# First product of the channel mixer by seven half products per pair of column blocks, with weight sums made partly by adding DMAs

## Chip, cores and metric

The kernel runs on one core of a Trainium2 chip. The metric is the device time of one launch in microseconds (us). The program names the engines as the profile does: PE is TensorE's matmul side, PEld its weight load, DVE is VectorE, ACT is ScalarE, POOL is GpSimd, SP is SyncE, which issues most DMAs.

## What is computed

One layer of a streaming encoder on 512 tokens with 2048 channels: an RWKV-7 token mixer, then a ConvFFN channel mixer, each between two RMS norms and modulated by the vector c. The change is in the channel mixer:

```python
def _conv_ffn(h, w_in, conv_w, conv_b, w_out):
    u = _causal_dwconv(h @ w_in, conv_w, conv_b)     # w_in: 2048 x 11008, conv of width 3
    gate, val = jnp.split(u, 2, axis=-1)             # 5504 columns each
    return (jax.nn.silu(gate) * val) @ w_out         # w_out: 5504 x 2048
...
    h = _rms(x, norm_ffn_pre[layer]) * (1 + sc_f) + sh_f
    f = _conv_ffn(h, ffn_w_in[layer], ffn_conv_w[layer], ffn_conv_b[layer], ffn_w_out[layer])
    x = x + g_f * _rms(f, norm_ffn_post[layer])
```

## The kernel before

Everything is float32 with channels on the partitions and tokens along the free dimension. A matrix product is made from 128x128 weight blocks and a 128x512 piece of the activations. Each float32 operand is split in two float32r parts, a high one (`wh`, `xh`) and the rest (`wl`, `xl`), and a block product is three matmuls: `wh`·`xh`, `wh`·`xl`, `wl`·`xh` (L246 to L248, function `mm3`). The 512 tokens are one matmul of 512 columns, or in some stages two halves of 256 (`HS`).

Weights come in 512 KB chunks of eight blocks (`w_load`, L188, issued on SP, three buffers `wr`). `w_split` makes half a chunk at a time into `wh` (a cast on ACT, L201) and `wl` (a subtraction on DVE, L203), with four buffers each, two to three halves ahead of PE.

The end of the program has these stages:

- The last six column blocks of `w_o` for half of the tokens, then for the other half (192 block products of 256 columns in all). Behind each half runs `between(h)`: norm, residual and pre-norm. Per row block it needs two DVE operations on `yo` (L1099, L1100), a square on ACT, an addition to `accx` on POOL (L1106), then a scaling on POOL (`ht`, L1116), the modulation on ACT and the split to `h2` (ACT, then DVE `xl`, L1121). At its end it stores the residual `yo` to `d_x1` by SP.
- The first three pairs of column blocks of `w_in` (a pair is block j of the gate and block j of the value) for each half of the tokens (288 matmuls of 256 columns for a half).
- Pairs 3 to 42 one after the other: 2 blocks x 16 row blocks x 3 = 96 matmuls of 512 columns a pair (`kinner`). `hidden` then makes the conv and the gating from PSUM: `conv` is one ACT and two DVE operations a block (L1157 to L1159), then silu on ACT and a DVE product into `act[j]` (L1167), which stays in SBUF. Meanwhile, from 1399 to 1525 us, `ada_jobs` multiplies the last sixth of `ada_w` by c on DVE (64 loads of 256 KB, L463).
- The product with `w_out` (`fo`): two runs of six column blocks of 512 columns, then a run of four in two halves of 256 columns, each over the 43 `act` rows, whose splits (L1246, L1247) are made four ahead. Then the last norm.

The kernel is written with a scheduling layer: the code's order is a wish, and each engine's queue is made from it ahead of time; on the chip each engine takes its queue strictly in order.

## Time and profile before

| | |
|---|---|
| median of 3 runs | 2770.28 us (2768.21 to 2771.6) |
| profiled execution (its span) | 2772.9 us |
| PE busy | 2639.9 us (95%) |
| DVE busy | 1745.4 us (63%) |
| halves of w_o, second half | 1271 to 1315 us |
| first three pairs, first and second half | 1315 to 1364 us, 1364 to 1399 us |
| pair 3 | 1399 to 1421 us |
| pairs 4 to 42 | 1421 to 2273.5 us |
| product with w_out, 512 columns | 2273.5 to 2624 us |
| product with w_out, 256 columns | 2624 to 2754 us |

The span is 2.6 us (0.1%) above the median of the timed runs, so a sum made against the span is lowered by 2.6 us to be put beside them. A row's busy time of PE counts each matmul with its latency, so the spacing of matmuls, not their mean duration, gives the rate; it is had from the number of matmuls in a stretch.

### The profile page before, as it was taken

The numbers are of one execution on the slowest core, as the hardware profiler recorded it, in microseconds if no ns is written. First come the engines' busy times: TensorE is split into PE (matmuls) and PEld (weight loads), VectorE is DVE, ScalarE is ACT, GpSimd is POOL, SyncE is SP. The second block draws the span as 40 slices with busy tenths as digits, with TensorE's granted clock in tenths as the row PEclk, the third lists the DMA queues.
The fourth block names the chain that finished last, engine by engine and source line by source line (L and its number), as shares of the span: only waits on it lengthen the run. The fifth ranks groups of instructions, "written<-read, shape, count | busy, mean of one in ns | idle before, by whom it ended". The sixth has DMA issues, their size and how long they took to land.

```text
span 2772.9 us, 40666 instructions
## 1 busy us (share of the span) xinstructions
PE 2639.9 (95%) x14946; PEld 2186.3 (79%) x14946; DVE 1745.4 (63%) x2708; ACT 1175.1 (42%) x2078; POOL 669.3 (24%) x731
## 2 busy tenths in 40 slices
PE   5899999989999999999899999999999999999997
PEld 3568787767777887788888888888888888888896
DVE  6978688888677677578877444444444454344476
ACT  4442255554444555446742333333333343343464
POOL 3543013686788464303500000000000000000000
PEclk8999999999999999999999999999999999999998
...
GB/s 303 278 200 346 252 244 204 199 199 241 185 186 204 168 183 179 120 297 192 225 220 221 99 99 95 95 99 99 95 96 99 99 90 104 99 99 93 100 207 198
DMA packets 274039, 472.28 MB, mean 170 GB/s; under 512 B 121360, under 2 KB 150416, under 8 KB 269744
## 3 DMA queue, kind: packets, MB, share of 16 engines
...
q10 hardware_dynamic: 432, 0.72, 0.1%
...
## 4 chain that ended last, share of the span: by engine, by line
PE 69%; DVE 5%; DMA 2%; issue 1%; SPq 1%; ACT 1%; POOL 0%; DVEq 0%; ACTq 0%; POOLq 0%
PE bk L246 20%; PE bk L248 20%; PE bk L247 20%; PE bk L840 2%; PE bk L871 1%; DVE wl L203 1%; PE bk L788 1%; PE bk L821 1%; PE bk L863 1%; DMA out<-x1t 1%; DMA x1t<-d_x 1%; PE bk L780 0%; PE bk L771 0%; PE bk L760 0%; PE bk L761 0%
## 5 line engine op out<-in xcount | busy, mean ns | idle before, releaser
L246 PE MATMUL bk<-xh,wh 128*128 128x512 f32 (+1 forms) x3452 | 1271.1, 372 | 7.0 <-ACT wh L201 3.3
L247 PE MATMUL bk<-xl,wh 128*128 128x512 f32 (+1 forms) x3452 | 1271.3, 370 | 0.0
L248 PE MATMUL bk<-xh,wl 128*128 128x512 f32 (+1 forms) x3452 | 1253.7, 371 | 18.4 <-DVE wl L203 18.2
L203 DVE TENSOR_TENSOR wl<-wr,wh 128x512 fp32r<-128x512 f32 x830 | 598.3, 725 | 704.9 <-ACT wh L201 681.5
L201 ACT CAST wh<-wr 128x512 fp32r<-128x512 f32 x896 | 552.2, 621 | 1087.3 <-PE bk L247 1028.0
L246 PEld LDWEIGHTS bk<-xh,wh 128*128 128x128 f32 x3452 | 655.5, 190 | 120.0 <-ACT wh L201 4.6
L248 PEld LDWEIGHTS bk<-xh,wl 128*128 128x128 f32 x3452 | 644.9, 190 | 132.8 <-DVE wl L203 23.6
L247 PEld LDWEIGHTS bk<-xl,wh 128*128 128x128 f32 x3452 | 655.3, 190 | 108.1 <-issue 3.0
L1217 POOL TENSOR_TENSOR fo<-fo,rs 128x256 f32<-128x256 f32 x4 | 3.7, 916 | 1375.2 <-ACT rs L1082 1375.2
L463 DVE SCALAR_TENSOR_TENSOR ja<-js,cs,ja 128x512 f32<-128x512 f32 x165 | 123.4, 748 | 52.9 <-DMA js<-ada 51.9
L203 POOL TENSOR_TENSOR wl<-wr,wh 128x512 fp32r<-128x512 f32 x66 | 96.5, 1464 | 96.7 <-ACT wh L201 76.4
L1247 DVE TENSOR_TENSOR xl<-act,xh 128x512 fp32r<-128x512 f32 (+1 forms) x172 | 92.1, 552 | 25.0 <-ACT xh L1246 25.0
L460 POOL TENSOR_TENSOR js<-js,cs 128x512 f32<-128x512 f32 x75 | 85.5, 1144 | 86.1 <-DMA js<-ada 67.9
L461 POOL TENSOR_TENSOR ja<-ja,js 128x512 f32<-128x512 f32 x75 | 104.6, 1395 | 2.1
L1246 ACT CAST xh<-act 128x512 fp32r<-128x512 f32 (+1 forms) x172 | 84.7, 511 | 31.9 <-PE bk L248 31.8
L712 POOL TENSOR_TENSOR ix<-ix,it 128x31 f32<-128x31 f32 (+15 forms) x124 | 90.0, 726 | 6.3
L710 POOL TENSOR_TENSOR it<-ia,ix 128x31 f32<-128x31 f32 (+15 forms) x124 | 83.3, 671 | 23.0 <-DMA ia<-d_gs 8.7
L840 PE MATMUL bk<-rh,lh 128*128 128x128 f32 x512 | 77.6, 299 | 3.5 <-DVE qz L841 2.7
L840 PEld LDWEIGHTS bk<-rh,lh 128*128 128x128 f32 x512 | 67.1, 203 | 7.8 <-DVE qz L841 3.2
L871 PE MATMUL bk<-qz,sv 128*64 128x64 f32 x512 | 63.3, 242 | 8.4 <-DVE sv L867 6.8
L396 DVE SCALAR_TENSOR_TENSOR xm<-xx,vec,h 128x512 f32<-128x512 f32 x64 | 64.0, 1058 | 9.4 <-POOL xx L382 9.4
L869 ACT ACTIVATE sv<-bk,el 64x64 f32<-64x64 f32 x128 | 39.5, 308 | 69.5 <-PE bk L863 66.3
(207 smaller groups left out, 2571.2 us busy)
## 6 DMA issues: line engine op xcount, KB each, us to landing
wr<-w SPq DMA_DIRECT2D x448, 512.0 KB
js<-ada SPq DMA_DIRECT2D x256, 256.0 KB
...
```

What stands on the lines that cost most here:

```text
L201: S.copy(hi, r)
L203: ins = on.tensor_tensor(lo, r, hi.bitcast(F32), ALU.subtract)
L246: PE.matmul(out[:, cs], wh[0:kp, 0:m], xh[0:kp, cs], start=start, stop=False)
L247: PE.matmul(out[:, cs], wh[0:kp, 0:m], xl[0:kp, cs], start=False, stop=False)
L248: PE.matmul(out[:, cs], wl[0:kp, 0:m], xh[0:kp, cs], start=False, stop=stop)
L460: G.tensor_tensor(w, w, c.to_broadcast([P, QC]), ALU.mult)
L461: G.tensor_tensor(a, a, w, ALU.add)
L463: eng.scalar_tensor_tensor(a, w, c, a, ALU.mult, ALU.add)
L712: G.tensor_tensor(X[0:BLK, j + 1:32, 0:w], X[0:BLK, j + 1:32, 0:w], tv, ALU.add)
L840: PE.matmul(qb[:, c], LH[i][:, 4 * h + c], RH[i][:, :, 4 * h + c], start=True, stop=True)
L871: PE.matmul(yp[hv, c * HD:(c + 1) * HD], sv[:, i], qz[i][:, i, q], start=True, stop=True)
L1247: V.tensor_tensor(ahl[e][1][:, cs], act[f][:, cs], ahl[e][0][:, cs].bitcast(F32), ALU.subtract)
```

## The change

Pairs 4 to 42 (`JS`, 39 of them) are computed by a Strassen scheme on a 2x2 partition: the weights of a pair are four chunks, (gate, value) x (rows 0 to 7, rows 8 to 15 of the 16 row blocks), the activations four quarters, (rows 0 to 7, rows 8 to 15) x (tokens 0 to 255, 256 to 511). Instead of eight quarter products there are seven, each of 8 row blocks x 3 matmuls of 256 columns, 168 a pair. What goes with it:

- Sums of activations (`t1`, `t2`, `t3`, `tees`), made once from `yo`, which now keeps the modulated h, and split: eight DVE operations of 1024 elements and six splits of 1024. A fourth (`tee4`) is written over the second token half of `h2[0..7]` in eight splits of 256.
- Sums of weights, for each pair: `ss[0]` and `ss[1]` by a plain load on SP (L1278) and a second DMA on POOL that adds to it (L1279, `accum_op`); `s24` by two DVE additions of 1024 elements (`f_s2`, `f_s4`). Three chunks are also loaded raw (`f_raw`). So seven 512 KB transfers a pair come in place of four, two of them adding.
- Seven weight splits of 1024 elements a pair in place of four (`f_split`); every third goes into one buffer `wx` in one piece, the others in halves as before.
- Five operations of 256 elements a pair out of PSUM on DVE and two on ACT combine the products (`u2`, `u3`, `cv`, `cg`). `hidden` reads SBUF, one product later (`late`); its last product moves to POOL, and the result is stored to DRAM (`d_act`) by POOL, except two that stay.
- The product with `w_out` starts with the two kept rows and fetches the others from `d_act` eight rows ahead. `ada_jobs` of the last sixth moves into this stage. The pool of the channel mixer is closed before it, and the new pool `outp` takes its place.
- In `between`, the residual is stored per half row block by POOL (32 stores of 128 KB) in place of 16 of 256 KB by SP, and `xt` has four buffers, not six.

```diff
@@ between(h)
             V.scalar_tensor_tensor(y, y, gm[:, kt:kt + 1], rs2[:, cs], ALU.mult, ALU.mult)
-            V.tensor_tensor(y, y, xts[kt % 6][:, cs], ALU.add)
+            V.tensor_tensor(y, y, xts[kt % NX][:, cs], ALU.add)
+            G.dma_start(d_x1[kt][:, cs], y)
...
-        if h:
-            for kt in range(KT):
-                nc.sync.dma_start(d_x1[kt], yo[kt])
-                yield
@@ hidden(j, pg, pv)
-        act[j] = ap_.tile([P, T], F32, tag=f"act{j}", name="act")
-        V.tensor_tensor(act[j], ug, uv, ALU.mult)
+        kept = {FT - 3: "xh", FT - 2: "xl"}.get(j)
+        if kept:
+            act[j] = xp.tile([P, T], F32, tag=kept, name="act", bufs=XB)
+            G.tensor_tensor(act[j], ug, uv, ALU.mult)
+        else:
+            G.tensor_tensor(ug, ug, uv, ALU.mult)
+            G.dma_start(d_act[j], ug)
@@ the sums
+    def tees():
...
+        for i in range(2):
+            while made[1] < HK + (i + 1) * n:
+                yield
+            ya, yb = big[i], big[2 + i]
+            V.tensor_tensor(ya[:, :, H0], ya[:, :, H0], ya[:, :, H1], ALU.subtract)
+            yield
+            parts_of("t1", i, ya[:, :, H0])
...
+    def f_sums(j):
+        if j in JS:
...
+            for i, (one, other) in enumerate(((2, 3), (0, 2))):
+                nc.sync.dma_start(t[:, i], chunk(j, one))
+                G.dma_start(t[:, i], chunk(j, other), accum_op=ALU.add)
+    def f_s2(j):
...
+            V.tensor_tensor(s24[0][:, 0], ss[j % 2][:, 0], l11[j], ALU.add)
+    def f_s4(j):
+        V.tensor_tensor(s24[0][:, 1], s24[0][:, 0], l12[j], ALU.add)
+    def f_split(n):
...
+        if n % 3 == 2:
...
+            hi, lo = wx[0][:, 0], wx[0][:, 1]
+            S.copy(hi, src)
+            V.tensor_tensor(lo, src, hi.bitcast(F32), ALU.subtract)
...
+    def product(n, ps, start, stop):
+        for k, (wh, wl) in enumerate(ready_w.pop(n)):
+            xh, xl = moving(n % 7, k)
+            PE.matmul(ps, wh, xh, start=start and k == 0, stop=False, skip_group_check=True)
+            PE.matmul(ps, wh, xl, start=False, stop=False, skip_group_check=True)
+            PE.matmul(ps, wl, xh, start=False, stop=k == CH - 1, skip_group_check=True)
+            tick()
@@ the pairs
-    for j in range(NF, FT):
-        pq = []
-        for q in range(2):
...
-        silu = hidden(j, *pq)
+    for m, j in enumerate(JS):
...
+        f_sums(j + 1)
+        product(n, A, True, False)
+        S.copy(p1, A)
+        f_split(n + 3)
+        if late:
+            late()
+        f_raw(l11, j + 1, 0)
+        product(n + 1, B, True, False)
+        V.tensor_tensor(u2, B, p1, ALU.subtract)
+        f_split(n + 4)
+        f_s4(j)
+        product(n + 2, C, True, False)
+        f_split(n + 5)
+        product(n + 3, B, False, False)
+        V.tensor_tensor(u3, B, p1, ALU.subtract)
+        V.tensor_tensor(cv[:, H1], u3, C, ALU.subtract)
+        f_split(n + 6)
+        f_raw(l12, j + 1, 1)
+        product(n + 4, A, False, True)
+        S.copy(cg[:, H0], A)
+        f_s2(j + 1)
+        f_split(n + 7)
+        product(n + 5, B, False, True)
+        V.tensor_tensor(cv[:, H0], B, p1, ALU.subtract)
+        f_split(n + 8)
+        f_raw(l22, j + 1, 3)
...
+        product(n + 6, C, False, True)
+        V.tensor_tensor(cg[:, H1], C, u2, ALU.subtract)
+        f_split(n + 9)
...
+    exps(late())
+    ffn.close()
+    ap_ = ctx.enter_context(tc.tile_pool(name="outp", bufs=1))
@@ the product with w_out
+    def fetch_act(i):
+        if i < FT and act[rows[i]] is None:
...
+            nc.sync.dma_start(act[f], d_act[f])
```

Three places of the engines' queues show what stands where. The names in the rows are tiles; what is in brackets is what an instruction waits for (an engine's or a DMA queue's semaphore).

DVE, in the second half of the first three pairs. Before, splits of weights (`wl`) and of `h2` (`xl`) take turns:

```order
L1121 TENSOR_TENSOR xl<-hu,xh 128x256 [waits Activation_49]
L203 TENSOR_TENSOR wl<-wr,wh 128x512 [waits DMAHW4_49,PE_49,Activation_49]
L203 TENSOR_TENSOR wl<-wr,wh 128x512 [waits DVE_49,PE_49,Activation_49]
L1121 TENSOR_TENSOR xl<-hu,xh 128x256 [waits Activation_49]
L203 TENSOR_TENSOR wl<-wr,wh 128x512 [waits DVE_49,DMAHW5_49,PE_49,Activation_49]
```

Now the sums (L1215, L1220, L1225, L1230) and their splits (L1209) stand between them:

```order
L222 TENSOR_TENSOR wl<-wr,wh 128x512 [waits DMAHW4_49,PE_49,Activation_49]
L1209 TENSOR_TENSOR t1l<-yo,t1h 128x1024 [waits Activation_49]
L1151 TENSOR_TENSOR xl<-yo,xh 128x256 [waits Activation_49]
L222 TENSOR_TENSOR wl<-wr,wh 128x512 [waits PE_49,Activation_49]
L1151 TENSOR_TENSOR xl<-yo,xh 128x256 [waits Activation_49]
L1220 TENSOR_TENSOR yo<-yo 128x4x256 [waits Activation_49]
L222 TENSOR_TENSOR wl<-wr,wh 128x512 [waits DMAHW5_49,PE_49,Activation_49]
```

Twelve of these fourteen operations of 1024 elements stand ahead of the first weight split of pair 3's own chunks, among the weight splits of this stage.

DVE, in the middle of the pairs. Before, a pair is eight weight splits and five operations of the conv:

```order
L203 TENSOR_TENSOR wl<-wr,wh 128x512 [waits DMAHW0_49,PE_49,Activation_49]
L203 TENSOR_TENSOR wl<-wr,wh 128x512 [waits PE_49,Activation_49]
L1158 SCALAR_TENSOR_TENSOR uv<-bk_16792,fvec,uv 128x511 [waits Activation_49]
L1159 SCALAR_TENSOR_TENSOR uv<-bk_16792,fvec,uv 128x510 [waits DVE_49]
L1167 TENSOR_TENSOR act<-ug,uv 128x512 [waits DVE_49]
L203 TENSOR_TENSOR wl<-wr,wh 128x512 [waits DMAHW1_49,PE_49,Activation_49]
```

Now (with the buffers' numbers), from the end of a pair's fourth product to a little behind its sixth:

```order
L1373 TENSOR_TENSOR u3_14394<-bk4_19056,p1_14392 128x256 [waits PE_49]
L1374 TENSOR_TENSOR cv_19059<-u3_14394,bk5_19057 128x256 [waits DVE_49]
L1315 TENSOR_TENSOR wl_19201<-s24_14376,wh_19200 128x512 [waits Activation_49]
L1288 TENSOR_TENSOR s24_14376<-s24_14376,wr_19204 128x1024 [waits DMAHW0_49,DVE_49]
L1305 TENSOR_TENSOR wx_14386<-wr_19108,wx_14386 128x1024 [waits PE_49,Activation_49]
L1315 TENSOR_TENSOR wl_19260<-s24_14376,wh_19259 128x512 [waits PE_49,Activation_49]
L1382 TENSOR_TENSOR cv_19059<-bk4_19056,p1_14392 128x256 [waits PE_49]
L1315 TENSOR_TENSOR wl_19264<-s24_14376,wh_19263 128x512 [waits Activation_49]
L1182 SCALAR_TENSOR_TENSOR uv_19343<-cv_19059,fvec_68,uv_19343 128x511 [waits Activation_49]
L1315 TENSOR_TENSOR wl_19295<-ss_14357,wh_19294 128x512 [waits PE_49,Activation_49]
L1285 TENSOR_TENSOR s24_14376<-ss_14397,wr_19349 128x1024 [waits DMAHW2_49,DMASW2_49,DVE_49]
```

The sums of weights have been moved far ahead: the last row (`f_s2`) is that of the pair after the next one. It stands between the ends of a pair's sixth and seventh product and waits for that later pair's adding DMA (`DMASW2_49`).

SP, in the middle of the pairs. Before, one row stands for 140 weight loads:

```order
L188 DMA wr<-w 128x1024 x140
```

Now each pair has three raw loads and the two plain loads of the sums, in this order:

```order
L1269 DMA wr<-w 128x1024 [waits DMAHW0_49,DVE_49]
L1269 DMA wr<-w 128x1024 [waits DMAHW6_49,DMAHW1_49,DVE_49]
L1269 DMA wr<-w 128x1024 [waits DMAHW7_49,DMAHW2_49,DVE_49]
L1278 DMA ss<-w 128x1024 [waits DMASW2_49,DVE_49]
L1278 DMA ss<-w 128x1024 [waits DMASW4_49,DVE_49]
```

The third of them takes the buffer that a weight split of the running pair gives free, and the loads of the sums for the pair after the next one stand behind it. At the start of the product with `w_out` SP has:

```order
L207 DMA wr<-w 128x1024 [waits DMAHW4_49,DVE_49]
L1453 DMA act<-d_act_11476 128x512 [waits DMASW3_49,DMASW4_49,DMASW2_49,DMASW5_49,DMASW1_49,DMASW6_49,DMASW0_49,DMASW7_49,PE_49,Pool_49]
L1453 DMA act<-d_act_11477 128x512
L1453 DMA act<-d_act_11478 128x512
```

The first fetch of a row waits for PE, POOL and all eight queues of POOL's DMAs, which free the closed pool's memory.

## Rows read from the trace of the kernel before

**Rows 1.** Page: busy time by engine; and the chain that ended last.
```profile
PE 2639.9 (95%) x14946; PEld 2186.3 (79%) x14946; DVE 1745.4 (63%) x2708; ACT 1175.1 (42%) x2078; POOL 669.3 (24%) x731
...
PE 69%; DVE 5%; DMA 2%; issue 1%; SPq 1%; ACT 1%; POOL 0%; DVEq 0%; ACTq 0%; POOLq 0%
```

**Rows 2.** Stretches (start:end length, busy us of each engine with instructions, clock, DMA share, GB/s).
```profile
1271.50:1315.40 43.90, 37.43 (x294) 35.70 (x293) 39.31 (x66) 28.43 (x65) 21.30 (x21) 1.00 0.54 173
1315.40:1364.50 49.10, 39.44 (x295) 37.86 (x293) 43.40 (x71) 33.14 (x76) 30.36 (x31) 0.93 0.75 241
1364.50:1399.20 34.70, 34.58 (x288) 34.58 (x289) 25.84 (x42) 26.02 (x54) 7.98 (x11) 1.00 0.62 186
1399.20:1421.00 21.80, 21.80 (x98) 18.07 (x98) 21.43 (x35) 12.89 (x20) 0.00 (x0) 1.00 0.61 190
1421.00:2273.50 852.50, 852.50 (x3777) 706.35 (x3777) 396.49 (x578) 275.23 (x442) 0.00 (x0) 1.00 0.37 113
2273.50:2624.30 350.80, 350.80 (x1549) 290.49 (x1548) 145.99 (x221) 134.76 (x229) 0.00 (x0) 1.00 0.32 98
2624.40:2686.00 61.60, 61.60 (x515) 61.60 (x514) 44.68 (x90) 41.78 (x94) 0.00 (x0) 1.00 0.61 186
```

**Rows 3.** Groups by line, 1530 to 2250 us (busy us, mean ns, idle before).
```profile
L247 PE MATMUL bk<-xl,wh 128*128 128x512 f32 x1060 | 412.4, 389 | 0.0
L203 DVE TENSOR_TENSOR wl<-wr,wh 128x512 fp32r<-128x512 f32 x265 | 183.1, 691 | 416.1 <-ACT wh L201 416.1
L1158 DVE SCALAR_TENSOR_TENSOR ug<-bk,fvec,ug 128x511 f32<-128x511 f32 x33 | 24.8, 750 | 0.0
```

**Rows 4.** The same, 1364.5 to 1399.2 us.
```profile
L246 PE MATMUL bk<-xh,wh 128*128 128x256 f32 x96 | 26.5, 284 | 1.0 <-ACT wh L201 1.0
L203 DVE TENSOR_TENSOR wl<-wr,wh 128x512 fp32r<-128x512 f32 x27 | 21.1, 795 | 8.2 <-ACT wh L201 7.2 <-PE bk L248 0.8
```

**Rows 5.** The same, whole span, shapes apart.
```profile
L1247 DVE TENSOR_TENSOR xl<-act,xh 128x512 fp32r<-128x512 f32 x86 | 57.5, 686 | 23.6 <-ACT xh L1246 23.6
L1247 DVE TENSOR_TENSOR xl<-act,xh 128x256 fp32r<-128x256 f32 x86 | 34.6, 417 | 1.4 <-ACT xh L1246 1.4
L1246 ACT CAST xh<-act 128x512 fp32r<-128x512 f32 x86 | 51.3, 620 | 28.1 <-PE bk L248 28.1
L503 POOL DMA_DIRECT2D d_xr<-xm x16 | 8.7, 541 | 15.2 <-DVE xm L502 14.6 <-issue 0.3
L661 POOL DMA_DIRECT2D d_e<-v x16 | 14.2, 887 | 42.3 <-ACT wh L201 25.9 <-ACT v L272 16.2 <-issue 0.2
```

**Rows 6.** Timeline of PE behind its longest wait (start, us, idle before).
```profile
1344.75 1.23 PE L248 MATMUL bk<-xh,wl 128*128 128x256 f32 x4 [3.53 <-DVE wl L203]
1345.77 0.41 PE L246 MATMUL bk<-xh,wh 128*128 128x256 f32 x1
1345.99 0.41 PE L247 MATMUL bk<-xl,wh 128*128 128x256 f32 x1
...
1349.70 0.28 PE L247 MATMUL bk<-xl,wh 128*128 128x256 f32 x1
```

**Rows 7.** Stretches: busiest DMA, and one 512 KB weight load from its issue.
```profile
1200.00:1225.00 25.00, 25.00 (x116) 20.81 (x115) 18.46 (x29) 7.55 (x14) 0.00 (x0) 1.00 0.95 338
1703.60:1704.60 1.00, 1.00 (x7) 0.81 (x6) 0.03 (x1) 0.00 (x0) 0.00 (x0) 1.00 0.00 0
1704.60:1706.90 2.30, 2.30 (x12) 1.91 (x11) 0.69 (x1) 0.62 (x1) 0.00 (x0) 1.00 0.69 228
```

**Rows 8.** Timeline of DVE and SP around that load.
```profile
1702.94 0.69 DVE L203 TENSOR_TENSOR wl<-wr,wh 128x512 fp32r<-128x512 f32 x1 [2.03 <-ACT wh L201]
...
1703.66 5.77 SPq L188 DMA_DIRECT2D wr<-w  x2
```

**Rows 9.** DMA issues by line (KB each, us to landing).
```profile
d_tn<-ix POOLq DMA_DIRECT2D x4, 512.0 KB, 4.6
...
d_tt<-ia POOLq DMA_DIRECT2D x4, 512.0 KB, 6.2
```

More of the change, by code (lines that the diff above doesn't have):

```diff
@@ L22 @@
 NL, NF = 6, 3
+NP = 1
 HS = (slice(0, T // 2), slice(T // 2, T))
@@ L178, in body @@
     mods = {q: cp.tile([P, KT], F32, name=f"mod{q}") for q in (2, 3, 4, 5)}
-    wst = {"load": 0, "split": 0, "use": 0, "raw": {}, "half": {}, "pool": 0}
+    wst = {"load": 0, "split": 0, "use": 0, "raw": {}, "half": {}, "pool": 0, "end": g.mid}
     def w_load():
         c = wst["load"]
-        if c >= g.nchunks:
+        if c >= wst["end"]:
             return
@@ L1179, in body, with chunk, f_raw @@
     nb = 2 * NF
-    jobs = ada_jobs(ap_, all_of(5), 7, (2,) * 6 + (1, 2), 3, last=True)
-    sides.append(jobs)
     for j in range(NF):
         hidden(j, pf[2 * j], pf[2 * j + 1])
-    for j in range(NF, FT):
+    JS = list(range(NF + NP, FT))
+    ss, s24, wx = {}, [], []
+    l11, l12, l22 = {}, {}, {}
+    def chunk(j, i):
+        return ap["w"][g.mid + 4 * (j - JS[0]) + i]
+    def f_raw(d, j, i):
+        if j in JS:
+            d[j] = wp.tile([P, CH * P], F32, tag="wr", name="wr", bufs=3)
+            nc.sync.dma_start(d[j], chunk(j, i))
@@ L1185, in body @@
+    for j in range(NF, NF + NP):
         pq = []
@@ L1236, in body @@
         b0 += n
-    steps = [(f, run[4]) for run in runs for f in range(FT)]
+    rows = out_rows(FT)
+    steps = [(f, run[4]) for run in runs for f in rows]
+    place = {f: i for i, f in enumerate(rows)}
+    def fetch_act(i):
+        if i < FT and act[rows[i]] is None:
+            f = rows[i]
+            act[f] = ap_.tile([P, T], F32, tag=f"act{f}", name="act")
+            nc.sync.dma_start(act[f], d_act[f])
+    for i in range(8):
+        fetch_act(i)
     ahl = {}
@@ L1249, in body @@
     nb = 0
-    for r, (b0, n, h, end, cs) in enumerate(runs):
+    for r, (b0, n, h, end, cols) in enumerate(runs):
         pf = [bank((nb + i) % 8) for i in range(n)]
```

200 lines of the change are left out of this document (159 added, 41 removed).

## The prediction

> **What bounds the kernel now.** I read the page first: PE is busy 95% of the span and 69% of the chain that ended last lies on it; DVE, the next engine, has 63% [rows 1]. An average hides stages, so I then cut the end of the program into stretches [rows 2]. In the 852.5 us of pairs 4 to 42 PE never pauses, the clock is granted in full, DVE works 396 us and ACT 275 us, and DMA is at 0.37. PE alone sets the time there. The halves before it are different: between 1271 and 1364 us PE idles 6.5 and 9.7 us while DVE is at about 90%.
>
> The rate of PE has to be read from spacing. At 512 columns three lines of 1060 matmuls share 720 us [rows 3], 226.4 ns each, and 1548 in 350.8 us give 226.6 [rows 2]. So 96 matmuls of a pair take **21.75 us**. (The stretch of the pairs holds 3744 of these and some 33 tiny ones of `ada_jobs`, which make up the rest of it and move with `ada_jobs` at the same price.) At 256 columns, 514 matmuls take 61.6 us and 288 take 34.6 us [rows 2]: 120 ns, not half of 226.5. PEld is busy for all of these stretches, but for only 83% of the 512-column ones: with short matmuls the weight load is what PE waits on.
>
> **The pairs, on PE.** 168 matmuls at 120 ns are **20.16 us**, a gain of 1.59 us a pair (7%, where the operation count falls by 12.5%), 39 x 1.59 = **62 us**. By the Trainium skill (TensorE: Matmul & The Clock Gate, Back-to-back issue gap) matmuls of 256 and 512 columns stand 262 and 518 cycles apart, about 109 and 216 ns; as an estimate from that page the pair would fall from 20.7 to 18.3 us and the gain would be 94 us. The trace disagrees at both widths, and the measurement decides.
>
> **The pairs, on the other engines.** *DVE:* a split of 512 costs 0.69 us [rows 3]; 256 elements take 0.42 and 512 take 0.69 [rows 5], so 1024 about 1.22. Seven splits, on average 4.67 in halves and 2.33 whole: 6.4 + 2.8. Two additions for `s24`: 2.4. Five operations of 256: 2.1. Four of the conv at 0.75 [rows 3]: 3.0. Together 16.8 us in 20.16, 83%, where it was 46%. It stays hidden only if the queue's waits don't add up. In the queue DVE must wait for PE at `u2`, `u3`, `cv` and for `wx`, whose one buffer comes free with a product; laid out against products of 2.88 us each, the order has about 2 us of slack a pair, and splits are done two products before use. I take nothing. *ACT:* seven splits at most 1.24 us each (two of 0.62, [rows 5]) and some 2.5 us else: 11 of 20 us. *POOL:* one product and three DMA issues of 0.54 to 0.89 us [rows 5]: idle otherwise. *DMA:* 3.9 MB in 20 us are 195 GB/s; 338 were reached [rows 7].
>
> **The adding DMA** is what the trace of before does not show, and it lies in a loop. `f_s2` for the pair after next waits for it in DVE's strict order. Behind `f_s2` DVE needs 9.0 to 10.3 us (12 or 13 operations, by the prices above) to come to the split that frees the buffer of the last raw chunk; only then SP issues that chunk and behind it the plain load of `ss`; the add follows that load; `f_s2` follows the add. From SP's issue (1703.66, at the end of the DVE split) to the first byte 1.0 us [rows 7, 8]. Two loads of 512 KB one behind the other: 4.6 us at the pace of the lone one (2.3 us), 3.1 us at 338 GB/s [rows 7]. The add from issue to landing: plain POOL transfers of this size took 4.6 and 6.2 us [rows 9], and if its data take twice the 2.3 us, up to 8.5. The loop is 9.0 + 1.0 + 3.1 + 4.6 = 17.7 us at the least and 10.3 + 1.0 + 4.6 + 8.5 = 24.4 at the most. I take 9.4 + 1.0 + 3.9 + 5.5 = 19.8, just under PE's 20.16, since the rows that price the add come from stretches with other traffic. So the pair stays at 20.16, but with hardly any room.
>
> **The entries and exits**, all costs. (a) 32 stores of `d_x1` on POOL, 0.54 to 0.89 us each [rows 5], stand between its additions to `accx`; POOL is 21.3 of 43.9 and 30.4 of 49.1 us busy [rows 2], and each half's norm waits for the last addition. 16 stores delay it by 9 to 14 us, of which PE has cover for most of the wait: 4 us, between 0 and 14. Storing `d_x1` by SP goes; it was hidden. (b) In 1364 to 1399 us DVE has 25.8 us of work [rows 2]; twelve operations of 1.22 us raise it to 40.5 against 34.7: **+6**, between 0 and 10. (c) From the first weight split of pair 3 to the one that the second product needs stand 38 DVE operations (12 splits, 14 of the conv, 8 of `tee4`, 4 of 1024): 8.3 + 10.5 + 3.4 + 4.9 = 27.1 us, against 21.75 + 2.9 on PE: +2.5, between 0 and 8. `ada_jobs` on DVE, which filled this stretch (21.4 of 21.8 us, [rows 2]), leaves it; that is the room it uses. (d) The first fetched `act` row waits until the closed pool is free: the last pair's conv and silu (about 4.5 us), the POOL product and its store's landing (some 6), then its own load (2 to 3.3) and split (1.3), about 14 us. The two kept rows cover 36 matmuls, 8.2 us. +6, and 2 more because PE ran at half pace for about 4 us after a wait of 3.5 us (210 ns a matmul instead of 120, from 1345.77 until 1349.6, [rows 6]): **+8**, between 0 and 12. (e) `ada_jobs` in the `w_out` stage adds 48 us of DVE work beside 146 in 351 us, and its loads and the fetched rows 27 MB beside 98 GB/s [rows 2]: nothing; without that cover the pace of DVE would show, some 10 us.
>
> **Sum.** Against the profiled span: 2772.9 - 62 + 4 + 6 + 2.5 + 8 = 2731.4. The timed runs lie 2.6 us lower: **2728 us**, 1.5% faster.
>
> **Rivals.** *1, slower: the adding loop sets the pair.* If the data of an add take twice as long, 9.4 + 1.0 + 4.6 + 7 = 22 us a pair, 0.25 more than before: 2772.9 + 10 + 20.5 - 2.6 = **2801 us**. From 20.16 us on the loop eats the gain, and from 21.2 (the gain per pair equals the 20.5 us of entries over 39) the kernel is slower than before. For it: the loop's upper half lies there. Against it: a store from POOL moved the same bytes in 4.6 us in busier stretches. The Trainium skill (Collectives: The Full Stack, The bandwidth ceiling) puts a reducing DMA at half the rate of a copy, since it reads two sources; no row of before shows an add, and this rival is what that rule would do here. *2, DVE sets the pair.* Where POOL works beside it, a split took 0.795 us, not 0.691 [rows 4]; with 15% on all its work DVE needs 19.3 us, and with 1.5 us of waits for PE 20.8: 2772.9 - 37 + 20.5 - 2.6 = **2754 us**. For it: 83% in a strict queue. Against it: POOL works little in the pairs. *3, the entries hide.* PE idles in the halves already, and the scheduler has room before pair 3; with 5 us in all **2713 us**.
>
> **Chances.** Forecast 0.48, rival 1 0.25, rival 2 0.20, rival 3 0.07. About 0.2%, 5.5 us, is what a measurement can tell from no change. The forecast, rival 3 and nearly all of rival 2 are faster than that, some of rival 1 (loops of 20.8 to 21.3 us) falls within it: faster 0.72, same 0.06, slower 0.22. The range reaches from 2708 (most entries hidden) to 2787 (a loop of 21.6 us), and leaves out 0.07 below and some 0.13 above.
>
> **What would show it.** Right: in the pairs matmuls 120 ns apart, a pair in 20.2 us, PE without pauses, `f_s2` not waiting for POOL's DMA; DVE 80 to 85% there; pauses of PE near 1315 to 1365 us, at the second product of pair 4, and 8 us into the `w_out` stage. Wrong: PE pauses in every pair, released by a split behind `f_s2` (rival 1, with DVE idle before L1285) or by a split with DVE busy throughout (rival 2); or a matmul spacing other than 120 ns.

## The result

The changed kernel took **2797.94 us** (median of 4 runs, 2791.99 to 2807.16) where the kernel before took 2769.24 on the same chip (4 runs, 2764.53 to 2771.6): ratio 1.0103, 95% interval 1.0078 to 1.0129. It is 1.0% slower; forecast were 2728 us and 1.5% faster, range 2708 to 2787. The number is that of rival 1 (2801 us). Its mechanism was only half right, as the runs below show. Once the wait is taken away by one more buffer, the same scheme takes 0.9906 of the time before (0.9887 to 0.9926).

The page of the kernel after, busy time by engine and the chain that ended last, by engine and by line [rows 1]:

```profile
PE 2602.2 (93%) x17754; PEld 2283.0 (82%) x17754; DVE 2057.6 (74%) x3103; ACT 1323.3 (47%) x2313; POOL 840.9 (30%) x925
...
PE 32%; DMA 13%; DVE 9%; issue 5%; ACT 2%; POOL 0%; DVEq 0%; SPq 0%; ACTq 0%; POOLq 0%
DMA wr<-w 10%; PE bk L267 7%; PE bk L265 7%; PE bk L266 7%; PE bk L1330 4%; PE bk L1328 4%; PE bk L1329 4%; DVE wx L1305 2%; DMA js<-ada 2%; DVE wl L1315 1%; DVE wl L222 1%; DVE ja L482 1%; DVE uv L1183 1%; DVE yo L1128 0%; DVE ug L1182 0%
```

PE had 69% of the chain and has 32%. First by line is a transfer, `wr<-w`: the load of a raw weight chunk. All DMA together had 2% before. In stretches of the program (length, busy us of PE, PEld, DVE, ACT, POOL with instructions, clock, DMA share, GB/s), cut at the same matmuls in each kernel: up to the last `w_o` blocks; from there to the first product of pair 4, which is the entry; the 39 pairs; the rest. After:

```profile
0.00:1221.87 1221.87, 1131.35 (x7323) 896.50 (x7324) 933.96 (x1420) 563.22 (x974) 607.29 (x661) 0.98 0.69 221
1221.87:1428.60 206.73, 177.13 (x1266) 167.01 (x1265) 174.54 (x266) 123.88 (x257) 82.18 (x103) 0.92 0.67 215
1428.60:2284.70 856.10, 808.75 (x6554) 798.78 (x6554) 646.53 (x889) 409.93 (x654) 142.91 (x152) 0.99 0.64 176
2284.70:2796.00 511.30, 484.96 (x2618) 420.73 (x2616) 302.57 (x530) 226.30 (x429) 8.54 (x10) 0.98 0.53 178
```

The pairs, where 62 us were to be gained, take 856.1 us against 852.5 before [rows 2]: 21.95 us a pair, not 20.16. 39 x 20.16 = 786.2 us, so 69.9 us are lost there. 47.4 us of them are time without a matmul (856.10 less 808.75). Of the other 22.5 us, some 8 are still the pauses (busy time counts each matmul with its latency, 0.28 us at a spacing of 0.12, so the starts before and behind a pause lie 0.16 us further apart than its idle time says). About 9 us are matmuls at half pace: behind six of the pauses some 100 matmuls in all stand 0.21 us apart. The rest is many short gaps. The entry is taken up behind the run of the kernel before that shows its own stretches. What PE and DVE waited for in the pairs (us, times, longest):

```profile
DVE s L1285 <- DMA wr<-w: 82.8, 37, 4.4
DVE s L1288 <- DMA wr<-w: 70.8, 28, 4.4
...
PE bk L1330 <- DVE wx L1305: 28.0, 14, 3.6
PE bk L1330 <- DVE wl L1315: 12.6, 15, 1.1
```

L1285 is `f_s2`, L1288 is `f_s4`. DVE stands still there for 153.6 us, 3.9 us a pair, and PE then waits for splits. Both are put down to a raw chunk (`l11` for `f_s2`, `l12` for `f_s4`), none to the adding DMA. One turn of the loop from one `f_s2` to the next, in order of time (start, us, engine, line, operation, idle before and its releaser):

```profile
1873.72 1.23 DVE L1285 TENSOR_TENSOR s<-ss,wr 128x1024 f32<-128x1024 f32 x1 [0.52 <-DMA wr<-w]
...
1880.55 0.85 POOL L1279 DMA_DIRECT2D ss<-w  x1 [17.87 <-DVE u L1367]
...
1881.11 0.33 SPq L1269 DMA_DIRECT2D wr<-w  x1
...
1883.60 0.90 POOL L1279 DMA_DIRECT2D ss<-w  x1
...
1886.67 0.68 DVE L1315 TENSOR_TENSOR wl<-wr,wh 128x512 fp32r<-128x512 f32 x1
...
1887.39 0.33 SPq L1269 DMA_DIRECT2D wr<-w  x1
...
1888.98 1.23 DVE L1288 TENSOR_TENSOR s<-s,wr 128x1024 f32<-128x1024 f32 x1 [1.62 <-DMA wr<-w]
...
1895.88 1.23 DVE L1285 TENSOR_TENSOR s<-ss,wr 128x1024 f32<-128x1024 f32 x1 [4.13 <-DMA wr<-w]
...
1899.27 1.22 DVE L1305 TENSOR_TENSOR wx<-ss,wx 128x1024 fp32r<-128x1024 f32 x1
...
1900.55 0.58 PE L1330 MATMUL bk<-t1h,wx 128*128 128x256 f32 x1 [2.81 <-DVE wx L1305]
```

The stretch behind that pause:

```profile
1900.55:1903.50 2.95, 2.95 (x14) 2.95 (x15) 2.95 (x6) 1.49 (x3) 0.00 (x0) 0.50 0.63 190
```

Read it as a loop. `f_s2` runs at 1873.72. DVE then works through its queue for 13.6 us until the split that ends at 1887.35 frees a raw buffer; SP loads it again at once (1887.39). Beside two adds (1880.55 and 1883.60) this load takes until 1895.9, 8.5 us, and the next `f_s2`, far ahead in DVE's queue, waits for just that chunk; by the trace, the add that it also needs had landed at 1888.7. `f_s4` at 1888.98 waited in the same way for the raw load issued at 1881.11. From one `f_s2` to the next it is 22.16 us. The split behind it comes late, PE pauses 2.81 us and runs at half pace until 1903.5, 14 matmuls in 2.95 us at a granted clock of 0.50, the lower of its two levels (1.2 GHz).

The turns are not all alike; three kinds follow one another. By the trace, 37 of the 38 turns between two `f_s2` end with the raw load; from an `f_s2` to the issue of that load it is 13.7 to 18.2 us, 15.9 in the mean (2.3 of it idle, mostly `f_s4` waiting for its own raw load), and the load takes 9.1 to 3.4 us, 5.9 in the mean. Over all raw loads of the pairs the median from issue to landing is 7.8 us. A plain load without adds beside it, some 20 us earlier, released POOL 3.9 us after its issue:

```profile
1854.90 0.33 SPq L1278 DMA_DIRECT2D ss<-w  x1
...
1858.83 0.85 POOL L1279 DMA_DIRECT2D ss<-w  x1 [17.54 <-DMA ss<-w]
```

With 3.9 us in place of 8.5 the turn shown would take 17.5 us, an estimate, under PE's 20.16.

### The profile page after: what moved, and what is told of

Read it like the earlier page. It is cut to its first block, busy times and chain, and to the rows that moved or that the text cites. A ratio compares the mean times of both kernels' runs of the same rounds, so it can differ in the third digit from the quotient of the medians.

```text
span 2796.0 us, 47774 instructions
## 1 busy us (share of the span) xinstructions
PE 2602.2 (93%) x17754; PEld 2283.0 (82%) x17754; DVE 2057.6 (74%) x3103; ACT 1323.3 (47%) x2313; POOL 840.9 (30%) x925
## 3 DMA queue, kind: packets, MB, share of 16 engines
q1 hardware_dynamic: 267776, 436.85, 49.2%
## 4 chain that ended last, share of the span: by engine, by line
PE 32%; DMA 13%; DVE 9%; issue 5%; ACT 2%; POOL 0%; DVEq 0%; SPq 0%; ACTq 0%; POOLq 0%
DMA wr<-w 10%; PE bk L267 7%; PE bk L265 7%; PE bk L266 7%; PE bk L1330 4%; PE bk L1328 4%; PE bk L1329 4%; DVE wx L1305 2%; DMA js<-ada 2%; DVE wl L1315 1%; DVE wl L222 1%; DVE ja L482 1%; DVE uv L1183 1%; DVE yo L1128 0%; DVE ug L1182 0%
## 5 line engine op out<-in xcount | busy, mean ns | idle before, releaser
L265 PE MATMUL bk<-xh,wh 128*128 128x512 f32 (+1 forms) x2204 | 782.2, 364 | 17.5 <-ACT xh L1150 5.0
L266 PE MATMUL bk<-xl,wh 128*128 128x512 f32 (+1 forms) x2204 | 786.2, 360 | 6.3 <-DVE xl L1151 6.3
L267 PE MATMUL bk<-xh,wl 128*128 128x512 f32 (+1 forms) x2204 | 768.3, 361 | 13.4 <-DVE wl L222 12.5
L220 ACT CAST wh<-wr 128x512 fp32r<-128x512 f32 x584 | 356.3, 619 | 525.4 <-PE bk L266 432.4
L222 DVE TENSOR_TENSOR wl<-wr,wh 128x512 fp32r<-128x512 f32 x518 | 386.4, 754 | 201.2 <-ACT wh L220 182.9
L1279 POOL DMA_DIRECT2D ss<-w x78 | 68.1, 873 | 689.6 <-DMA ss<-w 284.2
L1330 PE MATMUL bk<-xh,wl 128*128 128x256 f32 x832 | 237.5, 286 | 11.9 <-DVE wl L1315 11.9
L1328 PE MATMUL bk<-xh,wh 128*128 128x256 f32 x832 | 237.4, 285 | 3.8 <-DVE cv L1374 1.8
L1329 PE MATMUL bk<-xl,wh 128*128 128x256 f32 x832 | 236.4, 284 | 0.0
L1315 DVE TENSOR_TENSOR wl<-wr,wh 128x512 fp32r<-128x512 f32 x156 | 129.3, 853 | 1.3 <-ACT wh L1314 1.1
L1330 PE MATMUL bk<-xh,wx 128*128 128x256 f32 x416 | 118.6, 285 | 0.7 <-DVE wx L1305 0.5
L1328 PE MATMUL bk<-xh,wx 128*128 128x256 f32 x416 | 118.0, 284 | 0.0
L1329 PE MATMUL bk<-xl,wx 128*128 128x256 f32 x416 | 117.9, 283 | 0.0
```

The costliest lines, as they stand in the source:

```text
L220: S.copy(hi, r)
L222: ins = on.tensor_tensor(lo, r, hi.bitcast(F32), ALU.subtract)
L265: PE.matmul(out[:, cs], wh[0:kp, 0:m], xh[0:kp, cs], start=start, stop=False)
L266: PE.matmul(out[:, cs], wh[0:kp, 0:m], xl[0:kp, cs], start=False, stop=False)
L267: PE.matmul(out[:, cs], wl[0:kp, 0:m], xh[0:kp, cs], start=False, stop=stop)
L1279: G.dma_start(t[:, i], chunk(j, other), accum_op=ALU.add)
```

## Experiments on the pairs

Four explanations were open: the place of `f_s2` and `f_s4` in DVE's queue with the few raw buffers (A); the adding DMAs, as a load on the DMA engines or as a wait (B); DVE's amount (C); and, later, whether the loop goes through the raw load (R) or through the add itself (L).

**Without the adds** (`no_add`):

```diff
                 nc.sync.dma_start(t[:, i], chunk(j, one))
-                G.dma_start(t[:, i], chunk(j, other), accum_op=ALU.add)
```

> Leaves out the two adding DMAs of a pair (the sums hold their first chunk alone); the loads by SP, DVE's work and the products stay. In the changed kernel a pair takes 21.95 us where the matmuls alone are 20.16, and DVE stands idle 3.9 us a pair at f_s2 and f_s4, put down to the raw chunk's load. Theory A (place: f_s2 and f_s4 stand so far ahead in DVE's queue that the raw chunk, whose buffer comes free late, cannot have landed): the raw loads are issued as late as before, so most of the wait stays, pair 21.2 to 21.9 us, 2770 to 2795 us. Theory B (adding DMAs: beside them a raw load of 512 KB lands in 8.6 us where one alone takes 3.4): the wait is gone, pair 20.2 to 20.4, 2725 to 2735 us. Theory C (DVE has too much to do, 16.6 us a pair in a strict queue): pair 21.9, 2795 us.

Measured: 2740.17 us, the kernel before beside it 2779.74. The pairs take 786.75 us, 20.17 each. At the two sums (L1284 and L1287 in this kernel) DVE waits 6.8 us in all for raw chunks, 0.2 us a pair, and the median raw load takes 3.9 us:

```profile
1442.65:2229.40 786.75, 786.52 (x6553) 786.29 (x6552) 640.85 (x888) 416.80 (x654) 86.11 (x78) 1.00 0.43 142
```

C falls: DVE does 16.4 us a pair, nearly the 16.6 of the kernel after, and hides. B holds so far by the pairs; the time lies above its 2725 to 2735 us because the part of the program ahead of the change ended late here, at 1240.9 us.

**The same bytes by a plain transfer** (`plain_pool`):

```diff
-                G.dma_start(t[:, i], chunk(j, other), accum_op=ALU.add)
+                G.dma_start(t[:, i], chunk(j, other))
```

> The two adding DMAs of a pair become plain transfers of the same bytes by the same queue, at the same place and with the same waits (the sums then hold one chunk and are wrong). Theory B in its first form (adding is what costs): as without them, pair 20.2 to 20.5, 2725 to 2740 us, and the transfer lands in 3 to 5 us, not 9.1. Theory B in its second form (the bytes, or POOL's queue, cost): pair 21.5 to 22, 2780 to 2798 us, landing near 9 us. Theory A: 21.2 to 21.9, 2770 to 2795 us.

Measured: 2734.05 us (before 2779.74). 790.5 us for the pairs, 20.27 each. The expectation that a plain transfer lands in 3 to 5 us was wrong: it takes 7.2 us on this queue. The pair and the time are as B in its first form had them. Some of DVE's wait stays:

```profile
DVE s L1288 <- DMA wr<-w: 28.9, 22, 3.0
...
DVE s L1285 <- DMA wr<-w: 26.5, 30, 3.1
```

That is 1.4 us a pair in place of 3.9; PE waits for DVE for 2.5 us in all. The bytes alone make the raw loads late (6.45 us in the median), but not by enough.

**The two sums kept at their written place** (`pin`), with all adds:

```diff
-        V.tensor_tensor(u2, B, p1, ALU.subtract)
+        at = V.tensor_tensor(u2, B, p1, ALU.subtract)
         f_split(n + 4)
-        f_s4(j)
+        with tc.issue_after(at.ins):
+            f_s4(j)
...
-        V.tensor_tensor(cv[:, H1], u3, C, ALU.subtract)
+        at = V.tensor_tensor(cv[:, H1], u3, C, ALU.subtract)
...
-        f_s2(j + 1)
+        with tc.issue_after(at.ins):
+            f_s2(j + 1)
```

> Adding DMAs as they are; f_s4 is kept behind u2 of its own pair and f_s2 behind cv's second half, where the text has them, so that on DVE each stands 5 to 15 us later. Theory A: the raw chunk is there in time, DVE's idle time at f_s2 and f_s4 falls from 3.9 us a pair to under 0.5, pair 20.2 to 20.5, 2725 to 2740 us. Theory B (the loop over the adding DMA is itself 22 us long): the wait only moves, pair 21.5 to 22, 2780 to 2798 us. Theory C: pair 21.9, 2795 us.

Measured: 2736.34 us (before 2779.74); 788.0 us for the pairs, 20.2 each:

```profile
1438.20:2226.20 788.00, 786.52 (x6553) 786.30 (x6552) 662.80 (x891) 419.37 (x655) 143.85 (x152) 1.00 0.69 191
```

A holds as well, with the adds in full (DMA share 0.69, higher than the 0.64 of the kernel after, since the same bytes move in less time). So neither A nor B is the cause alone; the wait needs both.

**A fourth raw buffer** (`rot4`), taken in turn with the three:

```diff
+            if loads[0] % 4 == 3:
+                d[j] = ap_.tile([P, CH * P], F32, tag="wq", name="wq")
+            else:
-            d[j] = wp.tile([P, CH * P], F32, tag="wr", name="wr", bufs=3)
+                d[j] = wp.tile([P, CH * P], F32, tag="wr", name="wr", bufs=3)
+            loads[0] += 1
```

> A fourth buffer for the raw chunks, taken in turn with the three; nothing else is changed. Theory A in the form that the buffer is what comes late: raw loads are issued a third of a pair (7 us) earlier, DVE's idle time at f_s2 and f_s4 falls from 3.9 us a pair to under 1.5, pair 20.3 to 20.9, 2730 to 2755 us. Theory A in the form that the place on DVE alone matters, and theory B: SP's order puts the loads behind those of ss all the same, pair 21.5 to 22, 2780 to 2798 us.

Measured: 2734.34 us (before 2779.74); the pairs take 786.5 us, 20.17 each:

```profile
1436.00:2222.50 786.50, 786.45 (x6553) 786.24 (x6552) 646.76 (x887) 416.67 (x653) 138.36 (x152) 1.00 0.69 191
```

The buffer was the scarce thing: with the loads started earlier, `f_s2` and `f_s4` may stand where they are. DVE still waits 25.3 us at `f_s2` (0.6 a pair), which PE doesn't feel.

**The sums without their raw operand** (`no_raw`): three buffers, all loads and adds as in the kernel after, but `f_s2` and `f_s4` wait for no raw chunk.

```diff
-            V.tensor_tensor(s24[0][:, 0], ss[j % 2][:, 0], l11[j], ALU.add)
+            V.tensor_tensor(s24[0][:, 0], ss[j % 2][:, 0], ss[j % 2][:, 0], ALU.add)
...
-        V.tensor_tensor(s24[0][:, 1], s24[0][:, 0], l12[j], ALU.add)
+        V.tensor_tensor(s24[0][:, 1], s24[0][:, 0], s24[0][:, 0], ALU.add)
```

> The changed kernel with its three raw buffers, all loads and both adding DMAs of a pair; only f_s2 and f_s4 no longer read a raw chunk (each adds its first operand to itself, so the sums are wrong). Theory R (the loop that takes 21.95 us goes through the raw loads: a raw chunk is read by a split, its buffer is loaded again beside the adds in 5 to 9 us, and f_s4 or f_s2 waits for just that load): DVE's idle time at the two lines falls from 3.9 us a pair to under 1, the pair to 20.2 to 20.7 us, 2725 to 2750 us. Rival L (the loop goes through the adding DMA, issue to landing 9.1 us, and f_s2 waits for that as soon as the raw load is not later): f_s2 waits for POOL's transfer instead, pair 21.3 to 22 us, 2770 to 2798 us.

Measured: 2731.74 us (before 2769.36); 788.5 us for the pairs, 20.2 each, and the adds still land only 8.6 us after their issue:

```profile
1432.90:2221.40 788.50, 787.00 (x6553) 786.39 (x6552) 653.35 (x890) 419.32 (x654) 140.42 (x152) 1.00 0.70 191
...
ss<-w POOLq DMA_DIRECT2D x74, 512.0 KB, 8.6
```

DVE waits at neither line. R holds and L falls: the loop over the adding DMA, which the prediction had priced and rival 1 was built on, has room even with an add of 8.6 us. The loop that set the pair went through the raw load.

What an add costs the DMA engines can be read from three of these runs, from POOL's queue over the pairs (packets, MB, share of the 16 engines). Without adds, only the stores of `act` are on it:

```profile
q0 software_dynamic: 3040, 9.96, 3.4%
```

With the two transfers a pair as plain ones (`plain_pool`):

```profile
q0 software_dynamic: 13696, 48.77, 18.1%
...
ss<-w POOLq DMA_DIRECT2D x74, 512.0 KB, 7.2
```

And as adds (`pin`):

```profile
q0 software_dynamic: 13696, 48.77, 31.5%
...
ss<-w POOLq DMA_DIRECT2D x74, 512.0 KB, 7.9
```

The same packets and bytes take 31.5 - 3.4 = 28.1% as adds and 14.7% as plain transfers, 1.9 times as much engine time, while the landing grows only from 7.2 to 7.9 us (8.6 in `no_raw`, 9.2 in the kernel after). By the Trainium skill (Collectives: The Full Stack, The bandwidth ceiling) a reducing DMA runs at half the rate of a copy; the 1.9 in engine time agrees. By the Trainium skill (DMA: Bandwidth & Descriptors, Issuing engines are not separate DMA queues) transfers started by different engines run on the same 16 DMA engines and interleave; the raw load of SP that took 8.5 us beside POOL's adds agrees.

## Experiments on the entry and the end

**The kernel before once more** (`before_again`), for its stretches:

> The kernel before, once more, for its stages on this chip. In the two executions seen so far the first product's stage begins at 1421.06 us (before) and 1428.64 us (after), 7.6 us apart; but counted back by matmuls, the stretch from the last blocks of the mixer's output product to there took 184.8 us before and 206.8 after, and what lies ahead of it 1236.3 and 1221.9. If the part ahead only varies from execution to execution: it begins anywhere from 1222 to 1245 us here, the stretch takes 184 to 186 us again, and the entries of the change cost 22 us, not 7.6. If the change made the part ahead faster: it begins at 1236 to 1245 us here, where changed kernels stand at 1222 to 1241.

Measured: 2774.07 us (2771.4 beside it), and:

```profile
0.00:1235.96 1235.96, 1138.61 (x7323) 902.15 (x7324) 935.74 (x1422) 562.63 (x974) 602.63 (x661) 0.97 0.70 221
1235.96:1422.30 186.34, 172.66 (x1267) 166.57 (x1266) 158.35 (x257) 118.39 (x247) 59.58 (x62) 0.95 0.66 208
...
2275.00:2772.30 497.30, 477.56 (x2585) 415.37 (x2584) 256.32 (x453) 218.07 (x418) 6.68 (x8) 0.99 0.42 128
```

The entry takes 184.8 and 186.3 us in the two executions of before and 206.7 after: the change costs 20 to 22 us there, and not the 7.6 us that the starts of the pairs (1428.6 and 1421.06) suggest. In the six other executions here that have the same entry, with adds or plain transfers on POOL, it took 202.2 to 206.4 us, so 16 to 22 us over all. The part ahead of it, the same work in all kernels, ended at 1221.9 us in the execution of the kernel after and hid 14 us. In the other profiled executions of kernels with the change it ended between 1227 and 1241, six of the eleven by 1231, in both of before at 1236. That scatter is larger than most effects looked for here, so from here on stretches are compared, not times. Whether the change also makes that part a little faster is open.

The entry in four pieces, after (second half of the last `w_o` blocks; first three pairs, first and second token half; pair 3), for [rows 2]:

```profile
1258.69:1308.29 49.60, 38.85 (x291) 35.90 (x289) 39.75 (x66) 27.74 (x65) 24.61 (x36) 0.91 0.69 223
1308.29:1362.64 54.35, 40.35 (x289) 38.35 (x289) 46.62 (x72) 32.79 (x73) 35.45 (x46) 0.85 0.57 184
1362.64:1405.67 43.03, 38.43 (x288) 37.44 (x289) 39.06 (x50) 29.83 (x58) 15.70 (x16) 0.94 0.53 155
1405.67:1428.60 22.93, 22.93 (x97) 18.93 (x97) 19.61 (x31) 15.66 (x28) 6.41 (x7) 0.94 0.77 239
```

Before they took 43.4, 48.6 (50.1 in the second execution), 34.7 and 21.8: +6.2, +4.3 to 5.8, +8.4 and +1.1 us. In the same six other executions the third piece took 41.1 to 43.7 us and pair 3 21.6 to 22.8, so up to 3 and 1 us of these two costs are scatter.

Part of the third piece is the same effect as in the pairs. At its end PE stands for a cast that waits for a raw chunk:

```profile
1404.00 0.62 ACT L220 CAST wh<-wr 128x512 fp32r<-128x512 f32 x1 [4.87 <-DMA wr<-w]
...
1404.67 0.50 PE L265 MATMUL bk<-xh,wh 128*128 128x512 f32 x1 [2.63 <-ACT wh L220]
```

That chunk was issued at 1396.47, beside the first two adds (1395.98 and 1397.19), and took 7.5 us. In `no_add` this wait of PE isn't there, and the piece is the shortest of all kernels with the change:

```profile
1381.39:1421.11 39.72, 37.75 (x289) 36.97 (x290) 39.04 (x50) 29.43 (x58) 13.81 (x14) 0.94 0.46 150
```

**`d_x1` stored by ACT's queue** (`r4_act`, with four raw buffers):

```diff
-            G.dma_start(d_x1[kt][:, cs], y)
...
                 G.tensor_tensor(accx[:, cs], accx[:, cs], sq, ALU.add)
+            S.dma_start(d_x1[kt][:, cs], y)
```

> Four raw buffers, and the 32 stores of d_x1 issued by ACT's queue and not by POOL's. In the kernel with four raw buffers the two stretches of the halves take 50.2 and 53.8 us (43.4 and 48.6 before). Theory E1 (the stores stand between POOL's additions to accx and delay both norms): they fall to 44 to 47 and 49 to 51 us, and PE's waits for accx (6.7 us in two) fall under 3. Rival E2 (DVE's work or the two fewer x tiles set them): 49 to 51 and 53 to 55 us; or worse where ACT, busy 60% there, becomes the bound.

Measured: 2734.48 us (before 2771.4). The first three pieces (the fourth took 22.96 us):

```profile
1265.92:1309.79 43.87, 38.47 (x290) 36.74 (x289) 36.81 (x63) 26.56 (x61) 18.57 (x19) 0.96 0.73 225
1309.79:1361.82 52.03, 39.77 (x290) 38.50 (x288) 44.27 (x75) 33.83 (x77) 30.91 (x30) 0.89 0.64 206
1361.82:1411.00 49.18, 41.19 (x288) 39.16 (x288) 41.57 (x52) 31.12 (x60) 17.57 (x18) 0.90 0.60 181
```

The first piece is back at 43.9 us and PE's waits for `accx` are gone: E1 holds there. The second piece takes 52.0 us, where 53.8 were to become 49 to 51: little of it was the stores. And with four buffers alone the third piece took 43.3 us and now it takes 49.2; the sum of the four falls only from 170.0 to 168.0. So the gain is given back in the piece where DVE makes the token sums. What DVE does there is argued as the cause, not shown: it runs almost without a pause from 1361.8 to 1398, and it is slower beside POOL. While POOL works (first row) an operation of 1024 elements takes 1.75 us, with POOL idle 1.21; one of 256 takes 0.96 and 0.41. ACT also waits longer for raw chunks there, 11.5 us against 7.3 with four buffers alone.

```profile
1363.95 3.29 POOL L1146 TENSOR_TENSOR ht<-yo,rs 128x256 f32<-128x256 f32 x3 [0.17 <-ACT yo L1147]
1364.89 1.75 DVE L1215 TENSOR_TENSOR yo<-yo 128x1024 f32<-128x1024 f32 x1
...
1370.06 0.96 DVE L1151 TENSOR_TENSOR xl<-yo,xh 128x256 fp32r<-128x256 f32 x1
...
1374.11 0.41 DVE L1151 TENSOR_TENSOR xl<-yo,xh 128x256 fp32r<-128x256 f32 x1
...
1387.04 1.21 DVE L1230 TENSOR_TENSOR yo<-yo 128x1024 f32<-128x1024 f32 x1
```

**Second parts of the sums on POOL** (`r4_tp`, with four raw buffers): in `tees` alone

```diff
-            V.tensor_tensor(lo, src, hi.bitcast(F32), ALU.subtract)
+            G.tensor_tensor(lo, src, hi.bitcast(F32), ALU.subtract)
```

> Four raw buffers, and six of the fourteen large operations that make the token sums (the second parts, 1024 columns each) are done by POOL and not by DVE. The second half of the first product's first columns took 34.65 us before and 43.3 with four raw buffers, where PE waits for DVE's weight splits. Theory (DVE's amount sets it): 37 to 40 us. Rival (POOL's operations are slow and slow down DVE beside them, or delay h2): 43 us or more, and the first pair's second product may wait for the sums, 1 to 5 us more there.

Measured: 2740.12 us (before 2771.4); the third piece takes 47.8 us in place of 43.3, beyond its scatter. The rival holds: work given to POOL lengthens the piece.

**Half of the sums later, behind a second ordinary pair** (`r4_np2g`, with four raw buffers):

```diff
-NP = 1
+NP = 2
...
             while made[1] < HK + (i + 1) * n:
                 yield
+            while i and not go:
+                yield
...
     for j in range(NF, NF + NP):
+        if j == NF + NP - 1:
+            go.append(j)
```

(each step of `tees` is also kept behind the last weight split written before it.)

> Four raw buffers; two pairs in the ordinary way ahead of the seven-product ones and not one, and the second half of the token sums (seven operations of 1024 columns, 8.5 us of DVE) held back until the second of them. With four raw buffers the second half of the first columns takes 43.3 us with DVE at 90%, where PE needs 34.65, and the ordinary pair 22.8 where it needs 21.6. Theory (DVE's amount there sets the entry): the half takes 35 to 38.5 us, the two ordinary pairs 21.6 to 22.3 each; against four buffers alone the entry gains 5 to 8 us and the second ordinary pair costs 1.6, so 3 to 6 us less in all. Rival (the norm's latency and the weight splits set it, not the sums): 42 us or more, and 0 to 2 us more in all.

Measured: 2750.86 us (before 2769.36), of which 10 us is a slow first part (it ended at 1239.9). The third piece takes 40.9 us, between the 35 to 38.5 of the theory and the 42 of the rival; from the start of the entry to the end of the second ordinary pair it is 226.7 us, which is what four buffers alone need for the entry and their first seven-product pair (206.4 + 20.5). So nothing is gained in all, as the rival has it. With seven operations fewer the piece is 2.4 us shorter than with four buffers alone, hardly below its scatter (41.1 to 43.7), so DVE's amount is not what sets it.

**Both together** (`best`):

> Four raw buffers, d_x1 stored by ACT's queue, two ordinary pairs and the second half of the token sums held back. If the two cures of the entry add up (6 us in the first half by the stores, 5 to 8 in the second by the sums, less 1.6 for the second ordinary pair): 2720 to 2728 us where the kernel before takes 2770, ratio 0.982 to 0.985. If DVE's amount over the whole entry is what counts, so that a gain at one place is lost at the next: 2728 to 2735 us, ratio 0.985 to 0.987. In neither case slower than before.

Measured: 2737.72 us (median of 4, 2730.82 to 2744.98), ratio 0.9885 (0.9859 to 0.9912). The entry to the end of the second ordinary pair takes 222.0 us, 4.8 less than with four buffers alone, but the 38 pairs behind it take 3.4 us more and the rest 2.3. The cures don't add up, and the time lies above both expected ranges. What holds the third piece at 46.5 us there, with DVE busy for 34.6 of them, no run takes away. The trace has one candidate: ACT waits 11.6 us for raw chunks there, and PE's longest wait behind the start of the piece (2.80 us at 1402.95) is for a cast whose chunk took 9.1 us, while the second add was in flight (1391.90 to 1401.99).

**The last hidden unit kept in SBUF** (`r4_keep`, with four raw buffers):

```diff
-        kept = {FT - 3: "xh", FT - 2: "xl"}.get(j)
+        kept = {FT - 3: "xh", FT - 2: "xl", FT - 1: "xh"}.get(j)
```

> Four raw buffers, and the last hidden unit is kept in a slot of the first product's operand instead of going through memory. With four raw buffers alone PE stands still for 4.4 us where the first fetched act row is due; that row is asked for at 2230.95 us, 0.5 us behind the landing of the last store (2230.42, issued 2228.08), and the part from the end of the pairs to the end takes 510.0 us (499.4 before, about 4 us of it moved work). Theory X1 (the closed pool is free when that store has landed): the row is asked for 2.5 to 3 us earlier, PE's wait falls to 1 to 2 us, the part to 505 to 508. Rival X2 (another user of the pool, PE or DVE, is as late): no change within 1 us.

Measured: 2737.82 us (before 2771.4). With four raw buffers alone the first row is asked for at 2230.95, 8.4 us behind the end of the pairs (2222.5); a kept row had been split long before:

```profile
2218.30 1.29 DVE L1471 TENSOR_TENSOR xl<-act,xh 128x512 fp32r<-128x512 f32 x2
...
2228.08 0.59 POOL L1196 DMA_DIRECT2D d_act<-ug  x1 [0.30 <-POOL ug L1195]
...
2230.95 0.33 SPq L1458 DMA_DIRECT2D act<-d_act  x1
```

With the last unit kept, 5.2 us behind it (2223.6), at the end of POOL's product and not of a store:

```profile
2227.53 1.26 POOL L1193 TENSOR_TENSOR act<-ug,uv 128x512 f32<-128x512 f32 x1 [17.65 <-ACT ug L1188]
...
2228.82 0.33 SPq L1458 DMA_DIRECT2D act<-d_act  x1
2229.41 1.29 DVE L1471 TENSOR_TENSOR xl<-act,xh 128x512 fp32r<-128x512 f32 x2 [2.69 <-ACT xh L1470]
```

X1 is right on the fetch, which comes 3.2 us earlier. But the kept rows are now split only at 2229.41, probably because the kept unit took the slot that they were split into (argued from the edit, not shown), and PE stands 5.65 us in place of 4.43, at once behind the pairs. The part to the end takes 512.4 us against 510.0, not the 505 to 508 expected: nothing gained.

**The best simple version, timed** (`rot4_timed`, the kernel `rot4`):

> The kernel with a fourth raw buffer once more, against the kernel before in five rounds. If what its single run showed holds (39 pairs in 786 to 790 us, entry some 20 us and end some 10 us longer than before): 2728 to 2738 us, ratio 0.984 to 0.989, which is faster than both the kernel before and the changed one. If the single run was one of a wide scatter (a version with more changes ran from 2731 to 2745 us with the same pairs): median up to 2745 us, ratio up to 0.992, still faster than before.

Measured: 2742.49 us (median of 6, 2734.82 to 2745.09) against 2765.49 (11 runs): ratio 0.9906 (0.9887 to 0.9926). Pairs 790.8 us, entry 202.2, rest 515.3. The ratio is just above the expected 0.989 and within the 0.992 that a wide scatter was given; the median is 8 us above the first single run of the same kernel. It still beats the kernel before, and by the ratios the changed one.

## Why the prediction was wrong

- **The rate of PE, right.** 20.16 us a pair, within 0.01, in the kernels in which PE doesn't wait (`no_add` and `rot4`: 20.17).
- **The amounts, right.** DVE 646.5 us over 39 pairs is 16.6 us a pair (16.8 said), ACT 10.5 (11 said). Rival 2 falls: `no_add` has nearly the same DVE work and no loss.
- **"I take nothing" for DVE's waits, and the loop of 19.8 us: the step that failed.** The loop was drawn from `f_s2` over the release of a raw buffer, SP, the plain load of `ss` and the add, back to `f_s2`. The real one leaves it after the first load: `f_s2` itself reads the raw chunk that this load brings. Its row in the order names both waits (`DMAHW2_49` is that load, `DMASW2_49` the add), and only the second was read. The legs are 13.6 us of DVE (9.0 to 10.3 said) and 8.5 us for one raw load (1.0 + 3.9 said for the issue and both loads), 22.16 us in the turn shown, and 15.9 and 5.9 us in the mean of the turns. DVE's leg was too short because `f_s2` itself (1.23 us) was left out and because 16 operations stand behind it in the turn shown, not 12 or 13, one of them a split that takes 2.27 us in place of 0.69 beside POOL's product. The raw load was priced from a load alone on the queues [rows 7, 8]; beside the adds the median is twice that of `no_add` (7.8 and 3.9 us). `f_s4`, which waits nearly as much as `f_s2` (70.8 and 82.8 us), was not in the loop at all, although its wait for a load stood in the order.
- **The add, mis-sized, and harmless as a wait.** 5.5 us taken, 8.5 as the upper bound; 9.2 us measured in the kernel after. `no_raw` shows that an add of 8.6 us doesn't set the pair. It works through the DMA engines that it keeps busy, 1.9 times as long as a copy. So the sign "`f_s2` not waiting for POOL's DMA" came true although the forecast failed: it didn't look at the raw load.
- **Rival 1** gave the time (22 us a pair, 2801 us) and the sign to look for (DVE idle ahead of L1285). Its "if the data of an add take twice as long" was right as to engine time, its path wrong, so that the 22 us agree by luck: they are 9.4 + 1.0 + 4.6 + 7 there and 15.9 + 5.9 here. The time agrees partly by luck too. Against the profiled execution of before, the part ahead ended 14.4 us earlier, the entry cost 21.9, the pairs 3.6 and the rest 11.9, which makes 2796; rival 1 had 10 us for the pairs and 20.5 for all else. Its chance, 0.25, was too low for a loop whose upper half lay above 20.16.
- **The entries, too small.** (a) 4 us said, 10.5 to 12 measured (first two pieces), inside the 0 to 14; shown by `r4_act` to come from the stores in the first piece only. (b) 6 us said, 8.4 measured (6.4 to 9.1 over all), but by another way than DVE's amount alone: `no_add`, with the same DVE work, loses 5.1 there, `r4_np2g`, with seven operations fewer, 6.2, and 2.6 us of the loss are PE's wait behind the late raw chunk. (c) 2.5 said; pair 3 took 1.1 us longer, and at the second product of pair 4, near 1432 us, PE stands for 1.0 us in two waits. Together (a) to (c) 20 to 22 us in this execution against 12.5, which the span of one execution hid. (d) 8 us said: the rest grew from 499.4 to 511.3 us, of which 4.2 are the moved `ada_jobs` matmuls, so 7.7. Right within the scatter (the rest took 497.3 us in `before_again` and 508 to 515 in the other kernels whose end is unchanged). What releases the first fetch was right too (`r4_keep`: it comes earlier without the last store), but no run made the part shorter. (e) nothing said; no run separates it from (d).
- **The sum again** with the measured entry and without the wait: 2772.9 - 62 + 21 + 8 = 2740 us; the profiled execution of `rot4_timed` spans 2742.2. Term by term it agrees less well (entry 17.4, rest 11.7 besides the moved matmuls, pairs 4.6 slower than 20.16 each, the part ahead 2.3 shorter), so some of that is luck. (The prediction's own terms give 2728.8 us, which it wrote as 2728.)
